# A seven-form block product on one core: x4's weight sum moves from an accumulating load to VectorE, and the second product's forms come in another order

## The chip, the cores and the metric

One NeuronCore of a Trainium2 chip runs the whole program in one launch. The metric is the device time of one execution in microseconds (us); lower is better.

## The reference, cut to what matters

Two layers of a transformer trunk on 512 tokens of width 1024. The change lies in the dense block at the end of each layer, whose two matrix products are spoken of below as the first product (with `w_ff1`, 1024 x 4096) and the second product (with `w_ff2`, 4096 x 1024).

```python
for l in range(DEPTH):                       # DEPTH = 2, SEQ = 512, D_MODEL = 1024
    h = rmsnorm(x, attn_norm[l])
    ...                                      # two kinds of attention, output projection
    h = rmsnorm(x, mlp_norm[l])
    u = jnp.square(jax.nn.relu(jnp.einsum('bsd,df->bsf', h, w_ff1[l])))
    x = x + jnp.einsum('bsf,fd->bsd', u, w_ff2[l])
return rmsnorm(x, final_norm)
```

## The kernel before, in words

**Numbers as pairs.** Every operand of a matrix product is a float32 split into two parts, hi and lo. `split_part` does it for weights: ScalarE rounds a tile of 128 x 1024 raw weights to `whi` (line 114), VectorE subtracts to get `wlo` (line 130). `split` and `split_less` do the same for the activations (`Ah`, `Al`; lines 236, 237, 241, 242). `three` then issues three matmuls for each product: hi by hi, hi by lo, lo by hi (lines 296 to 298).

**Seven forms.** The dense block works through four groups of 1024 hidden columns (`g` 0 to 3). Within a group each product is cut in 2 x 2 blocks and done with seven block products instead of eight; these are the forms "11", "x3", "x2", "21", "x1", "x4", "22" of the list `FORMS`. A form's weights are a quadrant of the weight matrix or a sum of quadrants: x3 is 12 + 22, x2 adds 11 to that, x4 adds 21 to x2, x1 is 11 + 12. Its activations are a side of the same kind (`sides`, seven of them for each half `j` of a group). In group 0 the first product is done without forms (tiles `f`); in groups 1 to 3 it is `quad_group`, called for `j` = 0 and `j` = 1.

**The chains in PSUM.** The forms of a product are summed in PSUM: 11, x2, x1 and 22 in chain X, x3 in V, x4 in V too or, in the second product of groups 0 to 2, in W; 21 in Y. X is read out several times on its way: in the second product `gather` (line 1079 on VectorE; line 1077 on ScalarE where a result gets its first value) adds the two banks of X to the result `y` after 11, after x2, after x1 and after 22, so a matmul that goes on with X has to wait until the bank has been read. V and Y are read out in the last group alone (W after x4). In the first product VectorE reads X at line 1036.

**Weights of the second product.** Each form has two units of weights (`c` 0 and 1), 512 KB each, that lie in six tiles `kept` (`q` in the profile; the sixth is `waves`), by the table `HOME`: 11 and x1 in home 0; x3, x2 and x4 in home 1; 21 and 22 in home 2. A home's content grows in place. When a unit has been split, hooks (`then`) start the next load into its home: `grow` issues a load from GpSimd that adds a quadrant to what lies there (line 862; x1, x2 and x4), or from SyncE a plain load (line 860; 22). `fetch` loads 11, x3 and 21 of the next group. There are four pairs of `whi`/`wlo` tiles, so a unit is split at most four units ahead of its matmuls.

**Weights of the first product.** `bring` loads the quadrants of one `quad_group` into `first_a`, `first_b`, `first_c`, `waves` and `norms`; the sums are formed on VectorE by `add` (line 888): b += a gives x1, a += e gives x2, d += a gives x4.

**Order.** The code lists the work form by form; a scheduler of the framework then puts each engine's instructions in an order of its own, and semaphores are set by what is read and written. On the chip each engine goes through its instructions in that order and waits where one isn't ready. `rest_of_forms` makes the sides 21, x2 and 22 of both halves, which need the first product's form 22.

Of the kernel before, what the change touches and what calls it, by code (L numbers as in the profile page):

```python
# [39 lines left out]
TAIL, ATT, DENSE, CAP = 6.0, 53.0, 145.0, 0.1  # L40
FORMS = ("11", "x3", "x2", "21", "x1", "x4", "22")
SIDE = {"11": 0, "x4": 1, "21": 2, "x1": 3, "x3": 4, "x2": 5, "22": 6}
HOME = {"11": 0, "x1": 0, "x3": 1, "x2": 1, "x4": 1, "22": 2, "21": 2}
# [6 lines left out]
def _unit_list():  # L50
# [5 lines left out]
    for l in range(L):  # L56
# [13 lines left out]
        for g in range(GROUPS):  # L70
            if g == 0:
                units.extend(("1", l, f) for f in range(2 * GP))
            else:
                units.extend(("s", l, g, j, form) for j in range(2) for form in FORMS)
            for form in FORMS:
                for c in range(GP // 2):
                    units.append(("f", l, g, form, c))
# [85 lines left out]
def trunk(ctx, tc, opened, xT, w, w2, w1, gfin, lamv, cos, sin, out):  # L163
# [168 lines left out]
    for l in range(L):  # L332
# [502 lines left out]
        with ExitStack() as fctx:  # L835
# [21 lines left out]
            def grow(g, form, q, c):  # L857
# [3 lines left out]
                else:  # L861
                    nc.gpsimd.dma_start(t, quad(g, q, c), accum_op=ALU.add)  # L862

            def then(unit, fn, *args):
                W.then.setdefault(_INDEX[unit], []).append(lambda: fn(*args))
# [36 lines left out]
            for n, (g, j) in enumerate(groups):  # L902
                then(("s", l, g, j, "11"), add, "b", "a")
                then(("s", l, g, j, "x3"), add, "a", "e")
# [34 lines left out]
            def tt2(out, a, b, op):  # L939
                return nc.vector.tensor_tensor(out=out, in0=a, in1=b, op=op)  # L940
# [62 lines left out]
            def chunk(j, k):  # L1003
                return x[:, ((4, 5, 6, 7), (4, 5, 0, 1))[j][k], :]

            def quad_group(g, j, banks_):
# [8 lines left out]
                for form in FORMS:  # L1015
# [37 lines left out]
            def rest_of_forms(form):  # L1053
                for j in range(2):
                    F = [chunk(j, k) for k in range(4)]
                    hi, lo = ([e[:, k, :, :].rearrange("p a t -> p (a t)") for k in range(7)] for e in sides[j])
                    if form == "":
                        split_less(hi[5], lo[5], F[2])
                    elif form == "11":
                        split(hi[2], lo[2], F[3])  # L1060
                    elif form == "x3":
                        tt2(F[3], F[2], F[3], ALU.subtract)
                    elif form == "x2":
                        split(hi[6], lo[6], F[3])

# [97 lines left out]
            for g in range(GROUPS):  # L1163
                end = g == GROUPS - 1
                turn[0] = 0
                if g:
                    p_, q_, r_, s_ = r_, s_, p_, q_
                    quad_group(g, 0, (p_, q_, r_))
                    quad_group(g, 1, (s_, r_, q_))
                    rest_of_forms("")  # L1170
                else:
# [11 lines left out]
                chains = {"X": [temp(k, f"X{l}{g}{k}") for k in (p_, q_)], **held_on}  # L1183
                for form in FORMS:
                    total, to = SUMS[form], chains[CHAIN[form]]
# [49 lines left out]
                    if end and not last and form in ("x2", "21"):  # L1235
                        for c in range(4 * (form == "21"), 4 * (form == "21") + 4):
                            nc.sync.dma_start(x[:, c, :], park[c])
# [107 lines left out]
```

## Time and profile before

| | |
|---|---|
| median of 3 runs | 1140.46 us (1138.16 to 1142.93) |
| the profiled execution's own time | 1137.62 us |
| its span, first to last instruction | 1135.8 us |
| busy share of the span | TensorE 99%, VectorE 79%, ScalarE 60%, GpSimd 13% |
| accumulating loads of `grow` (line 862) | 48, 512 KB each |
| granted TensorE clock, mean | 0.997 |

Matmuls overlap in the profile: one of 512 columns is recorded with 0.39 us, while the next starts 0.227 us after it. A stall of TensorE is therefore read from the distance between the starts of two matmuls, and not from the idle time in brackets alone. Other engines overlap a little too: a row of VectorE that takes 1.23 us is followed by the next one after 1.14. Times within the profile are microseconds from the start of its span.

### The profile page before, as it was taken

How to read it: one execution, taken by the hardware profiler on the slowest of the kernel's cores; microseconds unless marked ns; L12 is line 12 of the kernel's file. 1: busy time of each engine (PE TensorE's matmuls, PEld its weight loads, DVE VectorE, ACT ScalarE, POOL GpSimd, SP SyncE). 2: the span in 40 equal slices, each digit the busy share in tenths (PEclk: the TensorE clock that was granted, in tenths of full speed). 3: DMA queues.
4: the chain of work that ended last, by engine and by line, in shares of the span. 5: the costliest groups of instructions: out<-in, count | busy, mean ns of one | idle time of the engine just before them, and what ended most of it. 6: DMA issues, size and time to landing. Idle time of an engine off the chain costs nothing.

```text
span 1135.8 us, 17692 instructions
## 1 busy us (share of the span) xinstructions
PE 1120.2 (99%) x6613; PEld 992.8 (87%) x6613; DVE 897.8 (79%) x1313; ACT 686.8 (60%) x1115; POOL 151.5 (13%) x237
## 2 busy tenths in 40 slices
PE   9999999999999999999999999999999999999997
PEld 7899889888889899898888998988888998988975
DVE  7897788789559778787888877887876787786876
ACT  6456666577558457466455565765773574764754
POOL 1000333101101101001000013330011010010010
PEclk9999999999999999999999999999999999999999
DMA  7665353266976857838327644522489679588282
GB/s 263 146 177 148 100 166 108 75 218 166 252 188 167 209 172 168 239 113 214 122 75 197 174 117 142 150 74 75 151 204 231 174 167 235 141 183 223 91 163 79
DMA packets 61621, 183.38 MB, mean 161 GB/s; under 512 B 7520, under 2 KB 8800, under 8 KB 61536
## 3 DMA queue, kind: packets, MB, share of 16 engines
q1 hardware_dynamic: 50160, 141.84, 39.4%
q0 software_dynamic: 10944, 39.85, 20.1%
q8 instruction: 52, 0.85, 0.3%
q10 hardware_dynamic: 432, 0.56, 0.1%
q14 instruction: 33, 0.27, 0.1%
HBM read 152.86 MB, written 4.19 MB: 138 GB/s over the span
## 4 chain that ended last, share of the span: by engine, by line
PE 82%; issue 8%; DMA 4%; DVE 3%; ACT 1%; POOL 1%; POOLq 0%; DVEq 0%; ACTq 0%
PE X L296 6%; PE X L297 6%; PE X L298 6%; PE wo L296 3%; PE wo L297 3%; PE wo L298 3%; PE f L298 3%; PE f L296 3%; PE f L297 3%; PE V L298 2%; PE V L297 2%; PE V L296 2%; DVE wlo L130 2%; PE Y L298 2%; PE Y L297 2%
## 5 line engine op out<-in xcount | busy, mean ns | idle before, releaser
L130 DVE TENSOR_TENSOR wlo<-q,whi 128x1024 fp32r<-128x1024 f32 x96 | 116.7, 1222 | 56.7 <-ACT whi L114 53.6
L114 ACT ACTIVATE whi<-q 128x1024 fp32r<-128x1024 f32 x96 | 100.8, 1056 | 91.7 <-DMA q<-in_w 28.0
L114 ACT ACTIVATE whi<-raw 128x1024 fp32r<-128x1024 f32 (+1 forms) x82 | 80.8, 993 | 50.4 <-issue 20.4
L130 DVE TENSOR_TENSOR wlo<-raw,whi 128x1024 fp32r<-128x1024 f32 (+1 forms) x82 | 95.2, 1168 | 12.1 <-ACT whi L114 11.6
L296 PE MATMUL X<-whi,Ah 128*128 128x512 f32 x248 | 97.8, 395 | 1.9 <-ACT whi L114 1.3
L297 PE MATMUL X<-wlo,Ah 128*128 128x512 f32 x248 | 97.4, 393 | 0.8 <-DVE wlo L130 0.8
L298 PE MATMUL X<-whi,Al 128*128 128x512 f32 x248 | 97.1, 391 | 0.0
L862 POOL DMA_DIRECT2D q<-in_w x48 | 42.4, 884 | 237.3 <-DVE wlo L130 223.9
L130 DVE TENSOR_TENSOR wlo<-waves,whi 128x1024 fp32r<-128x1024 f32 x40 | 48.9, 1222 | 17.1 <-ACT whi L114 17.1
L114 ACT ACTIVATE whi<-waves 128x1024 fp32r<-128x1024 f32 x40 | 42.3, 1057 | 32.7 <-PE X L298 16.6
L296 PE MATMUL X<-hxh,whi 128*128 128x256 f32 x192 | 54.6, 285 | 3.4 <-DVE x L1036 3.4
L296 PEld LDWEIGHTS X<-whi,Ah 128*128 128x128 f32 x248 | 46.9, 189 | 12.2 <-ACT whi L114 1.7
L297 PEld LDWEIGHTS X<-wlo,Ah 128*128 128x128 f32 x248 | 47.0, 190 | 10.4 <-DVE wlo L130 1.1
L298 PEld LDWEIGHTS X<-whi,Al 128*128 128x128 f32 x248 | 47.0, 189 | 9.9
L298 PE MATMUL X<-h_hi,wlo 128*128 128x256 f32 x192 | 54.3, 283 | 0.0
L297 PE MATMUL X<-h_lo,whi 128*128 128x256 f32 x192 | 54.3, 283 | 0.0
L298 PE MATMUL X<-hxh,wlo 128*128 128x256 f32 x192 | 54.3, 283 | 0.0
L297 PE MATMUL X<-hxl,whi 128*128 128x256 f32 x192 | 54.3, 283 | 0.0
L296 PE MATMUL X<-h_hi,whi 128*128 128x256 f32 x192 | 54.3, 283 | 0.0
L236 ACT ACTIVATE Ah<-x 128x512 fp32r<-128x512 f32 (+1 forms) x60 | 42.6, 710 | 16.5 <-DVE x L940 16.1
L296 PE MATMUL f<-h_hi,whi 128*128 128x512 f32 x128 | 50.3, 393 | 0.0
L298 PE MATMUL f<-h_hi,wlo 128*128 128x512 f32 x128 | 49.9, 390 | 0.0
(738 smaller groups left out, 3805.3 us busy)
## 6 DMA issues: line engine op xcount, KB each, us to landing
raw<-in_w SPq DMA_DIRECT2D x78, 512.0 KB, 3.7
q<-in_w POOLq DMA_DIRECT2D x64, 512.0 KB, 6.6
q<-in_w SPq DMA_DIRECT2D x48, 512.0 KB, 5.4
waves<-in_w SPq DMA_DIRECT2D x28, 512.0 KB, 5.5
first_a<-in_w SPq DMA_DIRECT2D x12, 512.0 KB, 3.8
first_b<-in_w SPq DMA_DIRECT2D x12, 512.0 KB, 4.8
first_c<-in_w SPq DMA_DIRECT2D x12, 512.0 KB, 3.5
norms<-in_w SPq DMA_DIRECT2D x12, 512.0 KB, 3.7
```

Of the source, the lines that this page charges most:

```text
L114: return self.nc.scalar.activation(o, src, AF.Copy)
L130: self.last = h, nc.vector.tensor_tensor(out=lo[:, a:b], in0=raw[:, a:b], in1=hi[:, a:b].bitcast(F32), op=ALU.subtract)
L236: a = nc.scalar.activation(hi, src, AF.Copy)
L296: nc.tensor.matmul(pt, ah, bh, start=first, stop=False, skip_group_check=goes_on)
L297: nc.tensor.matmul(pt, ah, bl, start=False, stop=False, skip_group_check=goes_on)
L298: nc.tensor.matmul(pt, al, bh, start=False, stop=last, skip_group_check=goes_on)
L862: nc.gpsimd.dma_start(t, quad(g, q, c), accum_op=ALU.add)
```

## The change

It has three parts. First, x4's weights are no longer made by an accumulating load of quadrant 21: `on_chip` adds the tile of 21, which still lies in home 2, to home 1 on VectorE, when x2 has been split; the load of 22 into home 2 follows that sum. Second, the second product goes through `FORMS2`, in which 21 comes before x2, and the sides are made in that order and half by half (those of `j` = 0 within the `quad_group` of `j` = 1). Third, in the first product the hook of b += a is hung on the split of x3 instead of that of 11.

```diff
+FORMS2 = ("11", "x3", "21", "x2", "x1", "x4", "22")
 ...
-            for form in FORMS:
+            for form in FORMS2:
                 for c in range(GP // 2):
                     units.append(("f", l, g, form, c))
 ...
+            def on_chip(g, c):
+                t = W.raw[_INDEX[("f", l, g, "x4", c)]] = kept[(1, c)]
+                nc.vector.tensor_tensor(out=t, in0=t, in1=kept[(2, c)], op=ALU.add)
 ...
-                then(("s", l, g, j, "11"), add, "b", "a")
+                then(("s", l, g, j, "x3"), add, "b", "a")
                 then(("s", l, g, j, "x3"), add, "a", "e")
 ...
-                    then(("f", l, g, "x2", c), grow, g, "x4", "21", c)
-                    then(("f", l, g, "21", c), grow, g, "22", "22", c)
+                    then(("f", l, g, "x2", c), on_chip, g, c)
+                    then(("f", l, g, "x2", c), grow, g, "22", "22", c)
 ...
+                    if j and form in ("11", "x3", "x2"):
+                        rest_of_forms(0, {"11": "21", "x3": "x2", "x2": "22"}[form])
 ...
-                    rest_of_forms("")
+                    rest_of_forms(1, "21")
 ...
-                    if g:
-                        rest_of_forms(form)
+                    if g and form in ("11", "x3"):
+                        rest_of_forms(1, "x2" if form == "11" else "22")
```

Where the instructions stand now. The numbers behind a name are those of the buffers; layer 1's groups are shown, and `waits` names the engine or queue that an instruction waits for.

**Place 1, TensorE at the end of x2.** In group 2 of layer 1, before, x2's last matmuls (chain X) and what follows:

```order
L297 MATMUL X_10332<-wlo_10374,Ah_1_8451 128x512
L298 MATMUL X_10332<-whi_10373,Al_1_8452 128x512
L296 MATMUL Y_8878<-whi_10390,Ah_1_8449 128x512 [waits Activation_49]
L297 MATMUL Y_8878<-wlo_10391,Ah_1_8449 128x512 [waits DVE_49]
L298 MATMUL Y_8878<-whi_10390,Al_1_8450 128x512
```

The same place now:

```order
L298 MATMUL X_10337<-wlo_10413,Ah_1_8451 128x512
L299 MATMUL X_10337<-whi_10412,Al_1_8452 128x512
L297 MATMUL W_10521<-whi_10464,Ah_1_8449 128x512 [waits Activation_49]
L298 MATMUL W_10521<-wlo_10465,Ah_1_8449 128x512 [waits DVE_49]
L297 MATMUL X_10336<-whi_10430,Ah_1_8449 128x512 [waits DVE_49]
L298 MATMUL X_10336<-wlo_10431,Ah_1_8449 128x512
L299 MATMUL X_10336<-whi_10430,Al_1_8450 128x512
L297 MATMUL X_10337<-whi_10430,Ah_1_8449 128x512 [waits DVE_49]
```

And now in the last group (group 3 of layer 1):

```order
L299 MATMUL X_11061<-whi_11140,Al_1_8452 128x512
L297 MATMUL V_8880<-whi_11192,Ah_1_8449 128x512 [waits Activation_49]
L297 MATMUL V_8881<-whi_11192,Ah_1_8449 128x512
L298 MATMUL V_8880<-wlo_11193,Ah_1_8449 128x512 [waits DVE_49]
L299 MATMUL V_8880<-whi_11192,Al_1_8450 128x512
L297 MATMUL V_8880<-whi_11192,Ah_1_8449 128x512
L298 MATMUL V_8880<-wlo_11193,Ah_1_8449 128x512
L297 MATMUL X_11060<-whi_11158,Ah_1_8449 128x512 [waits DVE_49]
```

Before, x2 (X) was followed by 21 (Y). Now x1, which goes on with X, is next, and its first matmul on each bank waits for VectorE; the scheduler has put two of x4's matmuls ahead of it in group 2, and six in the last group. In the other groups it is two, in group 0 of layer 0 one, in group 3 of layer 0 five.

**Place 2, VectorE in the last group.** `y<-V`, `y<-Y` and `y<-X` are the gathers of x3, 21 and of X. Before, from the split of 21 (`q_1_8448`) and of x2's second unit (`q_1_8447`):

```order
L130 TENSOR_TENSOR wlo_11115<-q_1_8448,whi_11114 128x1024
L130 TENSOR_TENSOR wlo_11098<-q_1_8447,whi_11097 128x1024
L1079 SCALAR_TENSOR_TENSOR y_1_8442<-V_8880,r_122,y_1_8442 128x512
L1079 SCALAR_TENSOR_TENSOR y_1_8442<-V_8881,r_122,y_1_8442 128x512
L940 TENSOR_TENSOR x<-x 128x512
L130 TENSOR_TENSOR wlo_11138<-waves,whi_11137 128x1024
L130 TENSOR_TENSOR wlo_11155<-q_1_8444,whi_11154 128x1024
L1079 SCALAR_TENSOR_TENSOR y_1_8440<-X_11055,r_122,y_1_8440 128x512
L1079 SCALAR_TENSOR_TENSOR y_1_8440<-X_11056,r_122,y_1_8440 128x512
```

Now, from the split of x2's second unit to the gather of x2:

```order
L131 TENSOR_TENSOR wlo_11141<-q_1_8447,whi_11140 128x1024
L238 TENSOR_TENSOR Al_1_8452<-x,Ah_1_8451 128x512
L867 TENSOR_TENSOR q_1_8447<-q_1_8447,waves 128x1024
L131 TENSOR_TENSOR wlo_11159<-q_1_8444,whi_11158 128x1024
L1084 SCALAR_TENSOR_TENSOR y_1_8441<-Y_8878,r_122,y_1_8441 128x512
L1084 SCALAR_TENSOR_TENSOR y_1_8441<-Y_8879,r_122,y_1_8441 128x512
L131 TENSOR_TENSOR wlo_11177<-q_1_8445,whi_11176 128x1024
L131 TENSOR_TENSOR wlo_11193<-q_1_8446,whi_11192 128x1024
L1084 SCALAR_TENSOR_TENSOR y_1_8440<-X_11060,r_122,y_1_8440 128x512
L1084 SCALAR_TENSOR_TENSOR y_1_8440<-X_11061,r_122,y_1_8440 128x512
```

The rows at line 867 are new. Both splits of x1 (`q_1_8444`, `q_1_8445`), the first one of x4 (`q_1_8446`) and the gather of 21 stand ahead of the gather of x2, where before the first split of x1 alone stood.

**Place 3, VectorE in the first product.** Around b += a of layer 1, group 3, before:

```order
L130 TENSOR_TENSOR wlo_10632<-first_b_8613,whi_10631 128x1024
L130 TENSOR_TENSOR wlo_10662<-waves,whi_10661 128x1024
L888 TENSOR_TENSOR first_b_8613<-first_b_8613,first_a_8607 128x1024
L130 TENSOR_TENSOR wlo_10692<-first_c_8662,whi_10691 128x1024
L130 TENSOR_TENSOR wlo_10725<-first_a_8607,whi_10724 128x1024
```

Now:

```order
L131 TENSOR_TENSOR wlo_10632<-first_b_8613,whi_10631 128x1024
L131 TENSOR_TENSOR wlo_10662<-waves,whi_10661 128x1024
L893 TENSOR_TENSOR first_b_8613<-first_b_8613,first_a_8607 128x1024
L131 TENSOR_TENSOR wlo_10692<-first_c_8662,whi_10691 128x1024
L131 TENSOR_TENSOR wlo_10725<-first_a_8607,whi_10724 128x1024
```

Nothing moved: the scheduler has put the sum at the same place.

More of the change, by code (lines that the diff above doesn't have):

```diff
@@ L1051, in quad_group, with rest_of_forms @@
                         nc.scalar.activation(F[3], F[3], AF.Square)
[L1053 to L1064, printed above, removed]
+                    if j and form in ("11", "x3", "x2"):
+                        rest_of_forms(0, {"11": "21", "x3": "x2", "x2": "22"}[form])
+            def rest_of_forms(j, form):
+                F = [chunk(j, k) for k in range(4)]
+                hi, lo = ([e[:, k, :, :].rearrange("p a t -> p (a t)") for k in range(7)] for e in sides[j])
+                if form == "21":
+                    split(hi[2], lo[2], F[3])
+                elif form == "x2":
+                    split_less(hi[5], lo[5], F[2])
+                elif form == "22":
+                    tt2(F[3], F[2], F[3], ALU.subtract)
+                    split(hi[6], lo[6], F[3])
             fresh = set() if last else set(y)
@@ L1183, in trunk @@
                 chains = {"X": [temp(k, f"X{l}{g}{k}") for k in (p_, q_)], **held_on}
-                for form in FORMS:
+                for form in FORMS2:
                     total, to = SUMS[form], chains[CHAIN[form]]
@@ L1232, in trunk @@
                         came = gather(total, to)
-                    if g:
-                        rest_of_forms(form)
-                    if end and not last and form in ("x2", "21"):
-                        for c in range(4 * (form == "21"), 4 * (form == "21") + 4):
+                    if g and form in ("11", "x3"):
+                        rest_of_forms(1, "x2" if form == "11" else "22")
+                    if end and not last and form in ("21", "x2"):
+                        for c in range(4 * (form == "x2"), 4 * (form == "x2") + 4):
                             nc.sync.dma_start(x[:, c, :], park[c])
```

## The prediction

> **What bounds the kernel now.** I read the busy shares first, to see which engine sets the pace.
>
> ```profile
> PE 1120.2 (99%) x6613; PEld 992.8 (87%) x6613; DVE 897.8 (79%) x1313; ACT 686.8 (60%) x1115; POOL 151.5 (13%) x237
> ```
>
> TensorE is busy for 99% of the span, and the change neither adds nor removes a matmul. So work taken from other engines is worth nothing by itself; what can change is the time that TensorE stands still. The list of waits says where that is, as total, times and longest, all in us:
>
> ```profile
> PE X L296 <- DVE x L1036: 3.4, 3, 2.4
> ...
> PE X L296 <- ACT whi L114: 1.3, 1, 1.3
> PE X L297 <- DVE wlo L130: 0.8, 1, 0.8
> PE X L296 <- DVE y L1079: 0.6, 1, 0.6
> ```
>
> Only the last three lie in the second product. The timeline gives their places, group 3 of layer 0 first, then group 3 of layer 1:
>
> ```profile
> 532.86 0.39 PE L298 MATMUL V<-whi,Al 128*128 128x512 f32 x1
> 533.80 0.47 PE L296 MATMUL X<-whi,Ah 128*128 128x512 f32 x1 [0.56 <-DVE y L1079]
> 534.11 0.40 PE L297 MATMUL X<-wlo,Ah 128*128 128x512 f32 x1
> ...
> 1090.02 0.39 PE L296 MATMUL V<-whi,Ah 128*128 128x512 f32 x1
> ...
> 1092.74 0.39 PE L296 MATMUL V<-whi,Ah 128*128 128x512 f32 x1
> 1093.16 0.50 PE L297 MATMUL V<-wlo,Ah 128*128 128x512 f32 x1
> ...
> 1098.35 0.39 PE L298 MATMUL X<-whi,Al 128*128 128x512 f32 x1
> 1100.05 0.51 PE L296 MATMUL X<-whi,Ah 128*128 128x512 f32 x1 [1.32 <-ACT whi L114]
> 1101.31 0.51 PE L297 MATMUL X<-wlo,Ah 128*128 128x512 f32 x1 [0.76 <-DVE wlo L130]
> ...
> 1101.89 0.62 PE L296 MATMUL X<-whi,Ah 128*128 128x512 f32 x1
> ...
> 1105.29 0.40 PE L298 MATMUL X<-whi,Al 128*128 128x512 f32 x1
> ```
>
> Undisturbed starts are 0.227 us apart (the twelve steps from 1090.02 to 1092.74 take 2.72), so a form of 24 matmuls takes 5.45. From the starts, the stall of layer 0 is 0.94 − 0.23 = 0.72, and about 0.08 for the longer step behind it (533.80 to 534.11). Those of layer 1 are 0.20, 1.48 and 1.03, and about 0.2 in longer steps behind them. Then eight steps, 1101.89 to 1105.29, take 3.40, or 0.425 each. The stretches of 5 and 6 us with the granted clock say why:
>
> ```profile
> 1094.00:1100.00 6.00, 4.74 (x21) 3.54 (x19) 3.90 (x5) 2.35 (x4) 1.19 (x2) 1.00 0.86 150
> 1100.00:1106.00 6.00, 5.19 (x15) 3.89 (x16) 5.97 (x7) 3.15 (x5) 0.88 (x1) 0.72 0.85 191
> ```
>
> The clock falls from 1.00 to a mean of 0.72, and the eight steps cost 0.20 more each, 1.6 in all. The last group loses 0.2 + 1.48 + 1.03 + 0.2 + 1.6 = 4.5, layer 0's 0.8.
>
> Both long waits have one origin, x2's accumulating load. ScalarE and VectorE show it:
>
> ```profile
> 531.16 1.23 DVE L130 TENSOR_TENSOR wlo<-q,whi 128x1024 fp32r<-128x1024 f32 x1 [3.76 <-ACT whi L114]
> 530.07 1.06 ACT L114 ACTIVATE whi<-q 128x1024 fp32r<-128x1024 f32 x1 [4.17 <-DMA q<-in_w]
> 1093.46 0.86 POOL L862 DMA_DIRECT2D q<-in_w  x1 [8.18 <-DVE wlo L130]
> 1098.94 1.06 ACT L114 ACTIVATE whi<-q 128x1024 fp32r<-128x1024 f32 x1 [3.65 <-DMA q<-in_w]
> ```
>
> In layer 0 the gather of 11 is queued on VectorE behind the split that waits for the load; in layer 1 TensorE waits for the split itself.
>
> **x2 one form later.** x2 now has 5.45 us more cover. In layer 1 the load issued at 1093.46 was split from 1098.94; x2 would begin at 1090.02 + 2 × 5.45 = 1100.9 instead of 1095.5. In layer 0 a split of 21, whose plain load comes much earlier, takes x2's place in VectorE's queue. So the 0.8 of layer 0 go, and of layer 1's 4.5 all but 0.3 at 1093.16, unless something else is late.
>
> **What is late in the last group.** I follow VectorE by its rows:
>
> ```profile
> 1090.75 1.22 DVE L237 TENSOR_TENSOR Al<-x,Ah 128x1024 fp32r<-128x1024 f32 x1
> 1091.89 1.22 DVE L130 TENSOR_TENSOR wlo<-q,whi 128x1024 fp32r<-128x1024 f32 x1
> ...
> 1094.76 1.41 DVE L1079 SCALAR_TENSOR_TENSOR y<-X,r,y 128x512 f32<-128x512 f32 x2
> 1096.08 0.68 DVE L237 TENSOR_TENSOR Al<-x,Ah 128x512 fp32r<-128x512 f32 x1
> 1096.68 1.22 DVE L130 TENSOR_TENSOR wlo<-q,whi 128x1024 fp32r<-128x1024 f32 x1
> ```
>
> A row of 1.22 occupies it for 1.14 (1090.75 to 1091.89), a side of 512 columns for 0.60 (1096.08 to 1096.68), a pair of gathers for 1.32 (1094.76 to 1096.08). The split at 1091.89 is that of x3's second unit; TensorE waited for it at 1093.16. Now the side of 21 stands ahead of it (0.60), so it begins at 1092.49, and the stall there grows from 0.3 to about 0.9. x2, the third form after 1090.02, then ends at 1090.02 + 3 × 5.45 + 0.9 = 1107.3.
>
> Between that split and the gather of x2 VectorE has seven splits and two sums of x4 (9 × 1.14 = 10.26), the gathers of 11 and of 21 (2 × 1.32) and of x3 (2 × 0.66), three rows of 0.60, and the first split of x4 (1.23): 17.25. It is done at 1092.49 + 17.25 = 1109.74. TensorE can do two of x4's matmuls after x2 with `whi` alone, to 1107.7, and stands until 1109.8 for `wlo`: 2.1, with 0.1 for the restart. By the end of the other four the gather is over (1109.62 + 1.32 = 1110.9 for both banks). Loss after: 0.9 + 2.1 + 0.1 = 3.1, against 4.5 before: **−1.4**. The bounds are −4.2 (VectorE has slack that my chain misses) and +0.2 (the clock falls again, 1.6).
>
> The Trainium skill, "TensorE: Matmul & The Clock Gate", Part 1, section "What's actually happening", has the clock fall to half after an idle window of about 3.4 us. This trace differs: two waits of 1.48 and 1.03 were enough. By the page a wait of 2.1 would leave the clock alone; by the row it may not, which is a rival below.
>
> **x1 right behind x2.** Both use X, so x1's first matmul on each bank waits for the gather of x2. Before, no gather of X was followed at once by X. What one needs is seen at the end of x1 in group 2 of layer 1, where W follows, and in group 0 of layer 0, where ScalarE gathers x2's X and Y follows:
>
> ```profile
> 1031.26 1.23 DVE L130 TENSOR_TENSOR wlo<-q,whi 128x1024 fp32r<-128x1024 f32 x1 [1.50 <-ACT whi L114]
> 1032.40 1.40 DVE L1079 SCALAR_TENSOR_TENSOR y<-X,r,y 128x512 f32<-128x512 f32 x2
> 1032.69 0.39 PE L296 MATMUL W<-whi,Ah 128*128 128x512 f32 x1
> ...
> 300.14 1.37 ACT L1077 ACTIVATE y<-X,r 128x512 f32<-128x512 f32 x2 [0.93 <-PE X L298]
> 300.62 0.39 PE L296 MATMUL Y<-whi,Ah 128*128 128x512 f32 x1
> ```
>
> The first bank's gather lasts 0.74 (1.40 less the 0.66 to the next), so it ends at 1032.40 + 0.74 = 1033.14, 0.45 after 1032.69, where X would go on. I assume the same split ahead of it, as the order has it (x4's first unit there). The two matmuls of x4 in between take 2 × 0.227 = 0.45. The bank is free just then; I add 0.08 for the signal and 0.08 for the restart (the excess of the step 533.80 to 534.11): 0.16. The second bank is free at 1.11, and wanted three matmuls later, at 0.61 + 0.68 = 1.29. Five groups (1 and 2 of layer 0; 0, 1 and 2 of layer 1) cost 5 × 0.16 = **+0.8**; the bounds are 0 and 5 × 0.61 = 3.1 (nothing covered). In group 0 of layer 0 the first bank (half of 1.37) is free 300.14 + 0.69 − 300.62 = 0.21 after, and one matmul (0.23) lies between; with signal and restart, **+0.1**. In group 3 of layer 0 five matmuls (1.13) cover 0.45: **0**, so its gain is **−0.8**.
>
> **x4 on VectorE.** Sixteen sums; the same operation on tiles of this size exists at line 888:
>
> ```profile
> 336.19 1.23 DVE L888 TENSOR_TENSOR first_b<-first_b,first_a 128x1024 f32<-128x1024 f32 x1 [5.62 <-DMA first_b<-in_w]
> 1026.00:1034.00 8.00, 8.00 (x37) 6.64 (x36) 4.88 (x6) 3.19 (x3) 0.89 (x1) 1.00 0.74 225
> ```
>
> 16 × 1.22 = 19.6 us more on VectorE, 2.3 in a group. In the 8 us of the second line VectorE is busy 4.88, so 3.1 are free; the split at 1031.26 came after 1.50 of idle, which ends with ScalarE and a freed slot, not with VectorE's load. **0** in seven groups; in the last its two sums are in the chain above. If the cover were gone it would cost 2.3 a group (a rival). The load of 22 follows the sum; before, it followed the split of 21, which came a form after x2's. It is issued about as before: 0. GpSimd's sixteen rows of 0.87 go, and GpSimd is 13% busy: 0.
>
> **b += a.** The order shows it at its old place, so its stalls (3.4 above) stay: 0.
>
> **The sum.** −1.4 − 0.8 + 0.8 + 0.1 = −1.3. The profiled execution's 1137.62 would be 1136.3. It lies 2.84 under the median of 1140.46, whose runs differ by 4.8 among themselves; on the median I forecast **1139.2**.
>
> **The rivals.** *The clock falls again.* In the last group TensorE stands 2.1 us in one piece.
>
> ```profile
> 339.53 0.28 PE L298 MATMUL V<-h_hi,wlo 128*128 128x256 f32 x1
> 342.20 0.39 PE L296 MATMUL X<-hxh,whi 128*128 128x256 f32 x1 [2.40 <-DVE x L1036]
> ```
>
> For it speaks 1101.89 to 1105.29 above; against it a wait of 2.40, after which the first product ran on without a slow stretch. +1.6: 1140.8.
>
> *VectorE becomes the bound (slower).* The first split of x4 is queued ahead of the gather of x2 on VectorE; each us by which it begins late is a us for x1. If the two sums are not absorbed in the three forms before, that is 2.3 in each of five groups, 11.4: 1139.2 + 11.4 = 1150.6; half absorbed, 1144.9. It decides from 1.5 of lateness, the idle at 1031.26. VectorE's 79%, and the last group, where I find it 2.1 late, speak for it; the 3.1 us free in 8 against it.
>
> *Fewer accumulating loads let the others land earlier.* b += a waits for its own load:
>
> ```profile
> DVE first_b L888 <- DMA first_b<-in_w: 20.7, 6, 5.6
> DMA to landing us min/median/max: 4.2/4.8/8.2
> 327.89 0.33 SPq L881 DMA_DIRECT2D first_b<-in_w  x1
> 296.96 0.88 POOL L862 DMA_DIRECT2D q<-in_w  x1 [2.19 <-DVE wlo L130]
> ```
>
> If that came in time, the 3.4 at line 1036 would go: 1139.2 − 3.4 = 1135.8. Against it: x4's loads are issued 30 us ahead (296.96, 327.89) and long over. The Trainium skill, "DMA: Bandwidth & Descriptors", section "Issuing engines are not separate DMA queues", says that loads of all issuers interleave on the same 16 engines, which would allow it only where both are under way.
>
> *The third edit does act*, through waits that the order doesn't show: the same 3.4 go, 1135.8.
>
> **How the numbers follow.** Forecast 0.50; clock 0.17; VectorE late by half 0.10, in full 0.13; loads 0.06; third edit 0.04. About 0.5% (5.7 us) is what a measurement of this kernel can tell from no change: 1134.8 to 1146.2. A fast rival passes it together with the last group's lower bound (1135.8 − 2.8 = 1133.0); I count half of the two, 0.05; of the slow ones the full one and a hundredth, 0.14; the rest, 0.81, is the same. The range from 1135 to 1146 holds all but the full VectorE case and those edges.
>
> **What would show it.** Right: no wait for `y L1079` at group 3 of layer 0; one wait of about 2 us for `wlo` at the end of x2 in the last group; at the ends of x2 in the middle groups steps of 0.3 to 0.5 before X; the three waits for `x L1036` unchanged. Wrong: waits of over 1 us for `y L1079` in the middle groups (VectorE is the bound), steps of 0.43 in the last group (clock), or shorter waits for `x L1036` (loads).

## The result and the profile after

The changed kernel took 1138.46 us (median of 22 runs, 1135.99 to 1140.70); the kernel before took 1139.35 (22 runs, 1134.09 to 1143.94). The ratio is 0.9988, with a 95% interval of 0.9977 to 0.9999. By that ratio it is 1.4 us faster, with an interval from 2.6 to 0.1; the two medians differ by 0.9. Forecast were 1.3 us.

The profiled execution took 1138.57 us, with a span of 1136.5, which is 0.7 longer than the span of before. The busy shares show the sixteen sums on VectorE and the sixteen loads that GpSimd no longer issues:

```profile
PE 1122.4 (99%) x6613; PEld 992.6 (87%) x6613; DVE 914.9 (81%) x1329; ACT 687.0 (60%) x1115; POOL 137.5 (12%) x221
```

VectorE has 17.1 us and 16 rows more, each of the new rows 1.22 us. The waits of TensorE in the second product and at the first product's read-out of X have become two lines:

```profile
PE V L298 <- DVE wlo L131: 2.6, 2, 1.9
...
PE X L297 <- DVE x L1041: 0.2, 1, 0.2
```

The waits for `y L1079` and for x2's splits are gone, as forecast, and those for `x` fell from 3.4 to 0.2, which was not. The timeline of the last group shows both waits of the forecast, at `wlo` of x3's second unit and at `wlo` of x4's first:

```profile
1091.98 0.39 PE L297 MATMUL V<-whi,Ah 128*128 128x512 f32 x1
1093.10 0.50 PE L298 MATMUL V<-wlo,Ah 128*128 128x512 f32 x1 [0.73 <-DVE wlo L131]
...
1106.61 0.61 PE L297 MATMUL V<-whi,Ah 128*128 128x512 f32 x2
1109.08 0.53 PE L298 MATMUL V<-wlo,Ah 128*128 128x512 f32 x1 [1.85 <-DVE wlo L131]
1109.42 0.61 PE L299 MATMUL V<-whi,Al 128*128 128x512 f32 x1
1109.83 0.63 PE L297 MATMUL V<-whi,Ah 128*128 128x512 f32 x1
1110.26 0.63 PE L298 MATMUL V<-wlo,Ah 128*128 128x512 f32 x1
```

The first is 1.12 − 0.23 = 0.89, the second 2.01 (from the second of the two matmuls in the row of 1106.61, which starts at 1106.84). Behind it eight steps are 0.41 to 0.43 long: in this execution the clock fell again. The granted clock, the third number from the end of a row, shows it:

```profile
1106.00:1109.40 3.40, 1.55 (x7) 0.98 (x6) 3.40 (x5) 2.33 (x5) 0.00 (x0) 1.00 0.32 131
1109.42:1112.83 3.41, 3.41 (x10) 2.64 (x9) 3.26 (x5) 0.00 (x0) 0.00 (x0) 0.50 0.02 5
```

In a middle group (1 of layer 0) the end of x2 looks like this:

```profile
385.43 0.39 PE L299 MATMUL X<-whi,Al 128*128 128x512 f32 x1
385.65 0.39 PE L297 MATMUL W<-whi,Ah 128*128 128x512 f32 x1
385.88 0.39 PE L298 MATMUL W<-wlo,Ah 128*128 128x512 f32 x1
386.22 0.50 PE L297 MATMUL X<-whi,Ah 128*128 128x512 f32 x1
386.55 0.39 PE L298 MATMUL X<-wlo,Ah 128*128 128x512 f32 x1
```

Two steps of 0.34 and 0.33 instead of 0.23: 0.22 us, in each of the five middle groups.

One thing in the profile was not in the forecast at all. The last matmul starts at 1126.83, before at 1127.49, and yet the span is longer. The end of the kernel hangs on another chain, which begins with the split of 22's first unit. Before (ScalarE, then VectorE):

```profile
1113.96 1.06 ACT L114 ACTIVATE whi<-q 128x1024 fp32r<-128x1024 f32 x1 [0.48 <-ACT x L1102]
1120.52 0.74 DVE L1079 SCALAR_TENSOR_TENSOR y<-V,r,y 128x512 f32<-128x512 f32 x1
```

And after:

```profile
1114.67 1.06 ACT L115 ACTIVATE whi<-q 128x1024 fp32r<-128x1024 f32 x1 [6.21 <-issue]
1121.22 0.75 DVE L1084 SCALAR_TENSOR_TENSOR y<-V,r,y 128x512 f32<-128x512 f32 x1
```

From that split to the end of the span it is 21.8 us in both. The split needs the tiles of x1's first unit, so it can't begin before the first half of x1 is done, and six matmuls of x4 now stand ahead of x1: 6 x 0.227 = 1.36 us of TensorE's work that was behind that point and is now ahead of it. From the start of the last matmul to the end of the span it is 8.31 us before and 9.66 after, a difference of 1.35.

### The profile page after: what moved, and what is told of

Read it like the earlier page. It is cut to its first block, busy times and chain, and to the rows that moved or that the text cites. A ratio compares the mean times of both kernels' runs of the same rounds, so it can differ in the third digit from the quotient of the medians.

```text
span 1136.5 us, 17656 instructions
## 1 busy us (share of the span) xinstructions
PE 1122.4 (99%) x6613; PEld 992.6 (87%) x6613; DVE 914.9 (81%) x1329; ACT 687.0 (60%) x1115; POOL 137.5 (12%) x221
## 4 chain that ended last, share of the span: by engine, by line
PE 88%; DVE 5%; DMA 2%; issue 2%; ACT 1%; SPq 1%; POOL 0%; POOLq 0%; DVEq 0%; ACTq 0%
PE X L297 8%; PE X L298 8%; PE X L299 8%; PE V L297 3%; PE V L298 3%; PE V L299 3%; PE wo L297 3%; PE wo L299 3%; PE wo L298 3%; PE f L297 3%; PE f L299 3%; PE f L298 3%; PE Y L298 2%; PE Y L297 2%; PE Y L299 2%
## 5 line engine op out<-in xcount | busy, mean ns | idle before, releaser
L863 POOL DMA_DIRECT2D q<-in_w x32 | 28.7, 898 | 177.9 <-DVE wlo L131 177.9
L298 PE MATMUL f<-h_lo,whi 128*128 128x512 f32 x128 | 49.8, 389 | 0.0
```

Source lines behind the costliest of these rows:

```text
L298: nc.tensor.matmul(pt, ah, bl, start=False, stop=False, skip_group_check=goes_on)
```

## The experiments

A number called an excess is, here and below, the distance between the starts of two matmuls less the usual one for their shape.

### The order alone

```diff
-                    then(("f", l, g, "x2", c), on_chip, g, c)
-                    then(("f", l, g, "x2", c), grow, g, "22", "22", c)
+                    then(("f", l, g, "x2", c), grow, g, "x4", "21", c)
+                    then(("f", l, g, "21", c), grow, g, "22", "22", c)
```

> The new order of the forms alone; x4 is made by accumulating loads again (48 at that line) and 22 is loaded after the split of 21. Theory L (the last group pays for the two sums on VectorE): the wait of 2.0 us for wlo of x4 in the last group falls under 1 us because VectorE's chain there is 2 x 1.14 = 2.3 us shorter, no slow steps of 0.43 us follow, and the kernel is 3 us below the changed one (ratio to before about 0.996). Rival (the wait comes from the order, not from the sums): wait and slow steps stay and the time is that of the changed kernel within 1 us. On the waits for x at the first product's read-out (4.2 us in the profile of before, 1.5 in that of the changed kernel): if the sixteen accumulating loads caused them, they are 3 to 5 us here; if their size is chance, anywhere from 1 to 5. At group 3 of layer 0 no wait of 0.7 us; at the ends of x2 in the middle groups about 0.2 us each.

Measured: 1149.02 us; ratio to before 1.0090 (1.0064 to 1.0117), 10 us slower. Both theories missed it. The new loss is one wait in group 0 of layer 0, of TensorE for `whi` of x4, and GpSimd's timeline there names its origin:

```profile
289.25 0.86 POOL L863 DMA_DIRECT2D q<-in_w  x1 [5.77 <-DVE wlo L131]
301.70 0.86 POOL L884 DMA_DIRECT2D norms<-in_w  x1 [11.58 <-PE Y L299]
302.26 2.12 POOL L863 DMA_DIRECT2D q<-in_w  x2
```

The third row holds both loads of x4. They stood behind a load into `norms` for the next group, before which GpSimd waited 11.58 us, until a matmul of 21 (Y). They landed so late that ScalarE waited 10.07 us and TensorE 7.0:

```profile
312.59 1.06 ACT L115 ACTIVATE whi<-q 128x1024 fp32r<-128x1024 f32 x1 [10.07 <-DMA q<-in_w]
```

With slow steps behind it this place cost about 9 us. In the old order two forms (21 and x1) lie between x2 and x4; now x4's first matmul comes right behind x2. So the sum on VectorE, which I had costed as a row to be hidden, takes x4 out of GpSimd's queue, and without it the new order is a loss.

### The sum on VectorE alone

```diff
 FORMS = ("11", "x3", "x2", "21", "x1", "x4", "22")     # the old order, for both products
-                    then(("f", l, g, "x2", c), grow, g, "x4", "21", c)
+                    then(("f", l, g, "x2", c), on_chip, g, c)
                     then(("f", l, g, "21", c), grow, g, "22", "22", c)
```

> The sum of x4 on VectorE alone, the forms in the old order and the third edit left out. The waits of the old order stay: 0.7 us at group 3 of layer 0, the two waits of 1.5 and 1.0 in the last group and its slow steps; the sums cost 0 in the middle groups and 0 to 2.3 us in the last one, so 0 to +2.3 us against before. If the sixteen accumulating loads caused the waits for x at the first product's read-out, these are about 1.5 us here and the time is 0 to 2.6 below before; if their size is chance, anywhere from 1 to 5.

Measured: 1144.29 us; ratio 1.0043 (1.0023 to 1.0063), 4.9 us slower, beyond what was expected. The waits show where:

```profile
PE X L296 <- DVE y L1083: 5.2, 5, 1.8
```

TensorE waits five times for the gather of 11 (0.6 in all before, once). In group 2 of layer 0 VectorE shows how it comes:

```profile
452.44 1.22 DVE L130 TENSOR_TENSOR wlo<-q,whi 128x1024 fp32r<-128x1024 f32 x1 [3.91 <-ACT whi L114]
453.58 0.68 DVE L242 SCALAR_TENSOR_TENSOR Al<-x,Ah 128x512 fp32r<-128x512 f32 x1
454.18 1.22 DVE L866 TENSOR_TENSOR q<-q,q 128x1024 f32<-128x1024 f32 x1
455.31 1.40 DVE L1083 SCALAR_TENSOR_TENSOR y<-X,r,y 128x512 f32<-128x512 f32 x2
```

The split of x2's first unit waits for its load, the sum comes right behind it, and the gather of 11, on which the first matmul of x2 waits, stands behind the sum: 1.13 us later than without it, with a load that was late anyway. The wait here is 2.00 us, and that in group 3 of layer 0 is 2.00 as well; behind the second one alone slow steps follow, 1.6 us in all.

### x4 of the last group by loads again

```diff
+                    if last and g == GROUPS - 1:
+                        then(("f", l, g, "x2", c), grow, g, "x4", "21", c)
+                    else:
                         then(("f", l, g, "x2", c), on_chip, g, c)
```

> The changed kernel with x4 made by accumulating loads in the last group of layer 1 alone. Theory L: as without the sums, the wait of 2.0 us for wlo of x4 falls under 1 us, the slow steps go, and the time is 3 us below the changed kernel (2.0 + 1.8, less what the load is late), ratio to before about 0.996. Rival: the load of x4, issued after x2's split, lands after VectorE would have been done, the wait stays at 2 us and the time too. The waits for x: as in the changed kernel (1.5) if the accumulating loads cause them, 1 to 5 if chance.

Measured: 1138.00 us; ratio 0.9981 (0.9966 to 0.9996), the changed kernel's time. The load into x4's home was issued at 1099.51 and ScalarE had the unit at 1106.77, behind two squares; the excess before x1 was 0.48 + 1.54 + 0.44 + 0.37, with slow steps behind it. The rival held (the load is no earlier than the sum), and the run doesn't tell whether VectorE's rows set the wait.

### The third edit undone

```diff
-                then(("s", l, g, j, "x3"), add, "b", "a")
+                then(("s", l, g, j, "11"), add, "b", "a")
```

> The changed kernel with the third edit undone (b += a hung on the split of 11 again). The scheduler puts every instruction where it stands in the changed kernel, so the time is the changed kernel's within 0.3%, and the profile is a second look at the same program: the last group's wait of 2.0 us and slow steps again. If the accumulating loads set the waits for x, they are 1 to 2 us again; if chance, they may be 3 to 5.

Measured: 1138.30 us; ratio 0.9985 (0.9968 to 1.0001), the changed kernel's. Its timeline is the same program a second time:

```profile
1105.97 0.61 PE L297 MATMUL V<-whi,Ah 128*128 128x512 f32 x2
1108.43 0.50 PE L298 MATMUL V<-wlo,Ah 128*128 128x512 f32 x1 [1.85 <-DVE wlo L131]
1108.78 0.40 PE L299 MATMUL V<-whi,Al 128*128 128x512 f32 x1
1109.02 0.40 PE L297 MATMUL V<-whi,Ah 128*128 128x512 f32 x1
```

The wait is 2.01 again, to the hundredth, and this time the clock did not fall. So the third edit does nothing, and a wait of 2 us is followed by a fall in one execution and not in another; the last section has what decides it.

### The sums of the last group on GpSimd

```diff
-                nc.vector.tensor_tensor(out=t, in0=t, in1=kept[(2, c)], op=ALU.add)
+                on = nc.gpsimd if last and g == GROUPS - 1 else nc.vector
+                on.tensor_tensor(out=t, in0=t, in1=kept[(2, c)], op=ALU.add)
...
+                        for step in weighed:
+                            behind(step, x2_read)
```

> The changed kernel, but in the last group of layer 1 the two sums of x4 are made on GpSimd instead of VectorE, with no new load; the final weighing of y on VectorE stays behind the gather of x2, as in the changed kernel. Theory L (VectorE's chain of 17 us sets the wait before x1): the chain is 2 x 1.14 = 2.28 us shorter, so the wait of 2.0 us for wlo of x4 is gone or under 0.3 us, no steps of 0.43 us follow in any execution, and the time is 2 to 3 us below the changed kernel's (about 1136). Rival: the sums on GpSimd are slow (its 128x512 multiply took 1.34 us, so about 2.6 us each) and late, x4's split waits for them, and the time is the changed kernel's or 1 us more.

Measured: 1139.70 us; ratio 1.0003 (0.9987 to 1.0018), no gain, and the wait grew (an excess of 2.96 + 1.03 before x1). Not because GpSimd was late. Here are GpSimd's two sums:

```profile
1097.34 2.39 POOL L868 TENSOR_TENSOR q<-q,q 128x1024 f32<-128x1024 f32 x1 [4.20 <-DMA q<-in_w]
1101.50 2.79 POOL L868 TENSOR_TENSOR q<-q,waves 128x1024 f32<-128x1024 f32 x1 [1.77 <-DVE wlo L131]
```

And VectorE's rows at the same time:

```profile
1098.48 1.80 DVE L946 TENSOR_TENSOR x<-x 128x512 f32<-128x512 f32 x1
...
1101.94 3.42 DVE L131 TENSOR_TENSOR wlo<-q,whi 128x1024 fp32r<-128x1024 f32 x1
1105.29 1.40 DVE L1085 SCALAR_TENSOR_TENSOR y<-Y,r,y 128x512 f32<-128x512 f32 x2
```

Rows that take 0.69 and 1.22 elsewhere took 1.80 and 3.42: they ended about one row's time after GpSimd's did (1099.73 and 1104.29). VectorE lost 1.1 + 2.2 us to save 2.3. Its gather of Y went back, ScalarE's squares waited for that (2.81 us), and `whi` of x4 stood behind them.

### The order with sums in one group

```diff
+                    if (l, g) == (0, 0):
                         then(("f", l, g, "x2", c), on_chip, g, c)
                         then(("f", l, g, "x2", c), grow, g, "22", "22", c)
+                    else:
+                        then(("f", l, g, "x2", c), grow, g, "x4", "21", c)
+                        then(("f", l, g, "21", c), grow, g, "22", "22", c)
```

> The new order with accumulating loads for x4 everywhere except in group 0 of layer 0, where the sums are on VectorE. The new order alone had a single wait of 7.0 us there, and 2 us more behind it, because both loads of x4 stood in GpSimd's queue behind a load that waited for its tile. Theory P (that place alone made the order slower): the wait goes, and the time is the changed kernel's, about 1138.5, 9 to 10 us below the order alone. Rival: VectorE sums are needed in other groups as well, and the time stays over 1142.

Measured: 1137.96 us; ratio 0.9991 (0.9972 to 1.0010). Two sums in group 0 of layer 0 take back the whole loss of the order alone, 11 us in the medians. In the other seven groups it makes no difference that these runs can tell which way x4 is made, as long as the order is the new one.

### The old order with the sums on GpSimd

```diff
-                nc.vector.tensor_tensor(out=t, in0=t, in1=kept[(2, c)], op=ALU.add)
+                nc.gpsimd.tensor_tensor(out=t, in0=t, in1=kept[(2, c)], op=ALU.add)
```

> The old order of the forms with the sums of x4 on GpSimd in all groups. Sums on VectorE in the old order cost 4 to 5 us: the waits for the gather of 11 (y) before x2 were 0.5, 2.0, 2.0, 0.3 and 0.6 us in five groups, where before had 0.7 in one. Theory Q (the sum stands ahead of the gather of 11 in VectorE's queue): on GpSimd it no longer does, these waits fall back to one of about 0.7, and the time is that of before within 1.5 us. Rival: x2's loads land late in the old order whatever engine sums, the waits stay, and so do the 4 to 5 us.

Measured: 1150.84 us; ratio 1.0098 (1.0069 to 1.0127). The waits for `y` are gone, so they did come from the sum's place on VectorE, but the time is 11 us over before: in their place stands

```profile
PE X L296 <- DVE x L1040: 10.0, 6, 2.4
```

VectorE reads X of the first product late in all six groups, and slow steps behind two of these waits cost another 2.8 us. GpSimd's sums (2.67 and 3.19 us on average) are long over by then. What VectorE waits for there is the load that b += a needs, 29.3 us in all instead of 20.7 before:

```profile
DVE first_b L892 <- DMA first_b<-in_w: 29.3, 6, 5.6
```

This kernel has as few accumulating loads of `grow` as the changed one, 32, and its loads into `first_b` land later there, up to 8.3 us after their issue. How the sums on GpSimd bring that about is not shown; what stands beside the late loads is in the next section.

### The kernel before, a second and a third time

> The kernel before once more, for a second profile. If the size of the waits for x at the first product's read-out is chance (a landing of 8.2 us in the first profile), they come to 1 to 3 us here instead of 4.2; if the sixteen more accumulating loads cause them, to 4 again. If the slow steps after the waits of 1.5 and 1.0 us in the last group are chance, they may be absent.

> The kernel before a third time, for its profile alone. Waits for x at the first product's read-out: 3.2 to 4.2 us again if they belong to the kernel (its sixteen more accumulating loads, or its order); 1 to 2 us would make them chance. Slow steps of 0.43 us in the last group: there in the first profile, not in the second; chance if they come and go.

Measured: 1136.14 and 1136.97 us in one execution each. The last group of the second:

```profile
1098.24 0.39 PE L298 MATMUL X<-whi,Al 128*128 128x512 f32 x1
1100.18 0.49 PE L296 MATMUL X<-whi,Ah 128*128 128x512 f32 x1 [1.55 <-ACT whi L114]
1101.44 0.50 PE L297 MATMUL X<-wlo,Ah 128*128 128x512 f32 x1 [0.77 <-DVE wlo L130]
1101.78 0.39 PE L298 MATMUL X<-whi,Al 128*128 128x512 f32 x1
```

The same two waits, somewhat longer than in the first profile, and no slow step behind them; none in the third profile either. The 1.6 us of slow steps that I counted for before were one execution's. The third profile has a fall at another place: behind the wait of 2.42 us at the first read-out of layer 0's group 1, where the first profile has a wait of 2.40 and no fall, fifteen steps of 0.21 instead of 0.12 cost 1.4 us. So the wait of 2.40 that I set against a fall was no evidence against it. The excess at the first product's read-outs of X, in all profiles:

| kernel | us in all |
|---|---|
| before, three profiles | 4.18, 3.25, 4.04 |
| sum alone; order alone; order with sums in one group | 3.62; 3.27; 3.69 |
| changed kernel, two profiles | 1.70, 2.32 |
| changed in the last group alone, four kernels | 2.03, 1.09, 1.54, 2.13 |
| old order with the sums on GpSimd | 11.7 |

The six profiles with both edits lie below all the others, which is hardly chance as a whole. Between before and the changed kernel most of it is one place, the first read-out of layer 0's group 1 (2.66, 0.35 and 2.69 us of excess, then 0 and 0.31): `first_b` was issued at 327.89 there and the sum began 8.3 us later, 8.3 again in the third profile of before, 6.0 in the second, and 5.5 and 5.6 in the two of the changed kernel. But the order alone, with all its loads, had 6.0 there, and the old order with the sums on GpSimd, with the fewer loads, waits the longest: the number of accumulating loads by itself does not set it. The traces show which load goes with it, one into `norms` that GpSimd issues when the earlier load into that tile has landed. The first row is of the first profile of before, the other two, with the load into `first_b` behind it, of the changed kernel:

```profile
327.19 0.87 POOL L883 DMA_DIRECT2D norms<-in_w  x1 [10.81 <-DMA norms<-in_w]
...
326.39 0.87 POOL L888 DMA_DIRECT2D norms<-in_w  x1 [10.02 <-DMA norms<-in_w]
329.06 0.33 SPq L886 DMA_DIRECT2D first_b<-in_w  x1
```

It was issued 0.70 us ahead of `first_b` (327.89) in the first profile of before, 1.15 in the third, 2.22 in the second, and 2.67 and 2.75 in the two of the changed kernel. In all 14 profiles there are 84 such loads, one ahead of the first read-out in each of the groups 1 to 3 of both layers. The six loads of `first_b` with less than 1.5 us between the two took 7.3 to 8.3 us to land, and the 78 others, with 1.9 us and more, 4.9 to 7.0. Two of the six are those of before, four are in the old order with the sums on GpSimd. No run moved this load by itself.

### The last group without its sums

```diff
-                nc.vector.tensor_tensor(out=t, in0=t, in1=kept[(2, c)], op=ALU.add)
+                if not (last and g == GROUPS - 1):
+                    nc.vector.tensor_tensor(out=t, in0=t, in1=kept[(2, c)], op=ALU.add)
...
+                        for step in (*squares, *weighed):
+                            behind(step, x2_read)
```

> The changed kernel without the two sums of x4 in the last group of layer 1 (quadrant 21 is left out of x4's weights there, nothing takes its place; squares and weighing of y stay behind the gather of x2). Theory L (the wait before x1 is the end of VectorE's chain): the chain is 2 x 1.14 = 2.28 us shorter, the wait of 2.0 us for wlo of x4 falls to 0.3 us or less, no steps of 0.43 us follow, and the time is 2 to 3.5 us below the changed kernel. Rival: something else holds that split or the gather (ScalarE, a slot), and the wait stays over 1 us.

Measured: 1134.80 us; ratio 0.9960 (0.9946 to 0.9974), 3.7 us below the changed kernel's median.

```profile
1107.81 0.50 PE L298 MATMUL V<-wlo,Ah 128*128 128x512 f32 x1 [0.33 <-DVE wlo L131]
1108.48 0.50 PE L297 MATMUL X<-whi,Ah 128*128 128x512 f32 x1 [0.16 <-DVE y L1085]
```

The excess before x1 fell from 2.01 to 0.49 + 0.44 (the wait for the split of x3's second unit was longer here, 1.11 instead of 0.89), with no slow steps. VectorE's chain sets the wait, which the run with loads in the last group could not tell from a late load. More is left than the 0.3 expected: the chain is 1.74 us shorter and not 2.28, because VectorE now stands idle for 0.44 ahead of the split of x2's second unit.

The 3.7 us (3.2 by the two ratios) are not all the wait's. The scheduler has put two of x4's matmuls ahead of x1 here instead of six, and from the last matmul's start to the end it is 8.81 us instead of 9.66. So the profiles show 1.1 us in the wait and 0.9 at the end; slow steps that come in some executions of the changed kernel may be the rest, which is not shown.

### The gather of 21 put back, and b += a behind the split of 11

```diff
-                        came = gather(total, to)
+                        if not (end and last and form == "21"):
+                            came = gather(total, to)
+                        if end and last and form == "x2":
+                            for step in gather(SUMS["21"], chains["Y"]):
+                                behind(step, came[1])
```

> The changed kernel with the gather of 21 (Y) of the last group of layer 1 put behind the gather of x2 on VectorE; everything is computed. Theory L: the chain ahead of x4's first split is one pair of gathers (1.32 us) shorter, the wait of 2.0 us falls to about 0.7, a fall of the clock behind it becomes unlikely, and the time is 1.3 us (without) to 3 us (with a fall avoided) below the changed kernel's. Rival: the wait stays at 2 us, or the pair that was put back delays the end by as much, and the time is the same.

Measured: 1135.18 us; ratio 0.9968 (0.9955 to 0.9980), 3.3 us below the changed kernel's median (2.3 by the two ratios) and 3.6 below before by the ratio. The excess before x1 is 0.92 + 0.44, without slow steps:

```profile
1106.38 0.39 PE L297 MATMUL V<-whi,Ah 128*128 128x512 f32 x1
1107.53 0.50 PE L298 MATMUL V<-wlo,Ah 128*128 128x512 f32 x1 [0.76 <-DVE wlo L131]
1108.19 0.50 PE L297 MATMUL X<-whi,Ah 128*128 128x512 f32 x1 [0.16 <-DVE y L1084]
```

Here too two of x4's matmuls stand ahead of x1 instead of six, and the end takes 9.03 us instead of 9.66, so that 0.6 us of the gain is the end's. This computes everything and is faster than before and than the changed kernel. The second one has in addition:

```diff
-                nc.vector.tensor_tensor(out=spots[to], in0=spots[to], in1=spots[by], op=ALU.add)
+                step = nc.vector.tensor_tensor(out=spots[to], in0=spots[to], in1=spots[by], op=ALU.add)
+                if to == "b":
+                    W.behind(step, W.last[1])
...
-                then(("s", l, g, j, "x3"), add, "b", "a")
+                then(("s", l, g, j, "11"), add, "b", "a")
```

> As the one with the gather of 21 put back, and b += a of the first product is forced on VectorE behind the split of 11 (two splits of 1.14 us go ahead of it), which the third edit names but the scheduler did not do. The waits for x at the first product's read-out, 1.1 to 2.3 us in the profiles of the changed kernel and its close relatives, fall under 0.5 us, since the load has 2.28 us more; time 1 to 2 us below the kernel with the gather put back alone. Rival: a += e and what follows moves back by as much, new waits come in its place, and the time is the same.

Measured: 1135.16 us; ratio 0.9968 (0.9954 to 0.9982), the time of the one without it. The excess at the read-outs of X went from 2.13 to 0.00; the span was 1 us shorter in its one profile, while the first wait of the last group grew from 0.90 to 1.41 + 0.25. The gain that was expected is not in the times.

## Why the prediction came out, point by point

The time was forecast within 1 us, and the shift within 0.1 us of that by the ratio. So close a hit is luck. The forecast time stands on a median of three runs of before, 1140.46, which 22 runs put at 1139.35; and of the terms, one is mis-sized and two were missed, with errors of both signs that cancel in part. Excess by stage, from the 1550th matmul (at 275 us, ahead of the first dense block) to the end, for the three profiles of before and the two of the changed kernel (the run with the third edit undone is the second; the attention of layer 1, 4.1 us in all five, is left out):

| stage | before | after | difference of means |
|---|---|---|---|
| layer 0, groups 0 to 2 | 2.66, 2.34, 4.34 | 1.06, 1.29 | −1.9 |
| layer 0, second product of group 3 | 0.80, 1.24, 0.49 | 0, 0 | −0.8 |
| layer 1, up to the last second product | 1.52, 1.45, 1.35 | 1.87, 2.27 | +0.6 |
| layer 1, last second product | 4.62, 3.27, 2.69 | 4.80, 3.00 | +0.4 |
| from the last matmul's start to the end | 8.31, 8.31, 8.32 | 9.66, 9.67 | +1.4 |

The sum is −0.3; the stretch as a whole goes from 860.35 to 860.21 in the means. The timed runs say −1.4, from −2.6 to −0.1, and the five profiles can't tell more. Falls of the clock are in these rows: 1.4 us in the 4.34 of the first row, and 1.6 each in the 4.62 and the 4.80 of the fourth.

**x2 one form later.** Right in place and size for layer 0: the waits for the gather of 11 are gone, −0.8 forecast, −0.8 measured.

**What is late in the last group.** Right on the chain: I had VectorE at work for 17.25 us from the split of x3's second unit to the end of x4's first split; it is 17.2 (1091.83 to 1109.02), the waits 0.9 and 2.1 became 0.89 and 2.01, and leaving the two sums out took the second wait down to 0.93. The term was still mis-sized, −1.4 forecast and +0.4 measured: I had subtracted from it a fall of the clock (1.6 us) that the profile of before happened to show. Two further profiles of before show none in the last group; of the two profiles of the changed program one does. Without the slow steps the row is 3.0 on average before and 3.1 after, so that the edits moved the waits of this group about and took nothing from them. The rival "the clock falls again" has no price of its own then: a fall comes or does not come on either side. The Trainium skill, "TensorE: Matmul & The Clock Gate", Part 1, section "What's actually happening", has the activity window run free, so that the same kernel meets it at different points; the two profiles of one program with the same wait agree with that. The idle window of about 3.4 us that the same section asks for does not agree: the falls here followed waits of 2.0, and of 1.5 and 1.0.

**The end.** Missing in the sum. I counted time at TensorE's last matmul, and the end hangs on the split of 22, which waits for x1's first half. The six matmuls of x4 that cover a part of the wait cost 1.36 us there. No run tried that by itself, but others bear it out. In five of them the scheduler has put two of x4's matmuls ahead of x1 (the order alone, the sums in one group, and three of the changes in the last group: x4 by loads, the sums on GpSimd, no sums). There too the split of 22 stands 21.8 to 21.9 us ahead of the end, and from the last matmul's start to the end it is 8.8 us; 8.31 + 2 x 0.227 is 8.76.

**x1 right behind x2.** +0.8 forecast in the five middle groups, 5 x 0.22 = 1.1 measured; +0.1 in group 0 of layer 0, 0.14 measured. The mechanism and the cover by x4's matmuls are as described; the signal and restart were 0.22 instead of 0.16.

**x4 on VectorE.** Costed at 0 in seven groups, which is right in the new order. But its cover was named for the wrong reason: I asked only whether VectorE had time. The sum's worth is that x4 leaves GpSimd's queue, 9 us in group 0 of layer 0, and its cost is its place in VectorE's queue, 4.9 us in the old order. Without the sums in group 0 of layer 0 the new order is a loss, and without the new order the sums are. The rival "VectorE becomes the bound" did not happen in the new order; it is what the sum alone shows.

**b += a, and the loads.** The third edit does nothing, as read from the order. The waits at line 1036 did not stay: 3.8 us on average became 2.0. That is the direction of the rival on fewer loads, with half of its price, but not by its mechanism: with the same fewer loads the old order with the sums on GpSimd waits 11.7 us there. A late landing goes with the load into `norms` close ahead; why that load comes earlier in the changed kernel stays open.

## What to carry to other kernels

Before a load is replaced by arithmetic, look at what stands ahead of it in its own queue, and at what will stand behind the arithmetic in the other one: here the two edits lost 10 and 5 us alone and gained together. Take a second profile of the kernel before, and do not book a gain on a stretch of slow clock that one execution shows. Follow the end of the kernel from its last output back; work moved ahead of the form that the end waits for costs its full time, even where it fills an idle engine.

## What the runs showed of the hardware

A VectorE operation with two operands in SBUF stood still while a GpSimd sum of 128x1024 ran: 3.42 us instead of 1.22 beside a GpSimd row of 2.79, and 1.80 instead of 0.69 beside one of 2.39. In the old order with the sums on GpSimd each of the sixteen sums held up one such row, 23 us in all. The gathers, whose other operand lies in PSUM, took their usual 0.74 to 0.75 beside the same sums. The Trainium skill, "SBUF — State Buffer", section "SBUF: two separate sides", calls the port pair that both share an exclusive lock, held for the whole instruction, and names a VectorE operation with two SBUF inputs among those that need it; the rows agree.

TensorE's clock fell behind a wait of 2.01 us in one execution and not in another of the same instructions; it cost eight steps of 0.2 us, 1.6 in all. In all the profiles, 14 of them, a fall that comes while TensorE has work left is to half and lasts 3.41 us (6.83 behind the wait of 7.0 us):

```profile
1101.89:1105.30 3.41, 3.41 (x10) 2.64 (x9) 3.41 (x5) 1.04 (x3) 0.60 (x1) 0.50 0.72 125
...
342.85:346.26 3.41, 3.41 (x19) 3.41 (x18) 2.44 (x3) 2.03 (x2) 0.00 (x0) 0.50 0.47 142
```

The first row is of the first profile of before, the second of its third. Within an execution the falls, with the last one behind TensorE's last matmul counted in, start a whole number of times 3.413 us apart: 1101.89 and 1132.61 in the first profile of before (nine times), 1109.42 and 1129.90 in the changed kernel (six times), 504.62 and 1071.23 in the old order with the sums on GpSimd (166 times). I cut each profile, from 20 us on, into steps on that grid and added up the time without a matmul in each. Every step with 1.84 us or more was followed by half clock, none with less than 1.60, and of the seven between two were. That answers the pair of executions with the same wait of 2.01: in the one its idle 1.85 us lie in one step, 1106.01 to 1109.42; in the other the grid, taken from its fall at 1128.22, cuts them at 1107.74 into 1.16 and 0.69. A wait of 2 us is followed by a fall when it lies within one step of the grid, and no edit of this case sets where it lies.
